# Fourier weight tiles loaded with 128 rows instead of 127, and the two special rows in one load

## The chip, the cores and the metric

The kernel runs on one core of one Trainium2 chip. The metric is the time of one launch in microseconds (us), as the device reports it; of several runs the median counts. Engines are named as the profile names them: PE (matmul; PEld is its weight load), DVE (vector), ACT (scalar), POOL (GpSimd) and SP, whose queue here issues nearly all DMAs.

## The reference, cut to what matters

A trunk of two layers works on 16 meta tokens and 1024 tokens of width 1024, L = 1040 positions in all. Each layer normalises, projects into four groups (pooling, Fourier, state space, attention), mixes each group, gates it, and adds an output projection of all four to the residual. The change touches the Fourier group alone:

```python
def fourier_mix(u, w):
    mixed = jnp.fft.fft2(u.astype(jnp.float32), axes=(1, 2), norm="ortho").real
    return jnp.einsum("blc,cd->bld", mixed.astype(u.dtype), w)
```

## The kernel before, in words

The transform over the 512 channels and the weight `w` (512x512) are both linear, so the kernel first folds them into one: `fft_tables` (L404) multiplies a cosine and sine table with `w`, and what it leaves, the tiles `s.mt` and the row `s.mn`, is the right side of the transform over channels in `fft_inner` (L443). Since the tables have symmetries, `fft_tables` needs only sums and differences of rows of `w`: row m with row 512 - m, and so on. The host lays out `w` for this as `fw`: four tiles of 128 rows per layer, tiles 0 and 2 in rising order, tiles 1 and 3 in the falling order of their partners. The partners of rows 0 and 256 are missing, so row 0 of tile 1 holds the special row 128 and row 0 of tile 3 the special row 384.

In each layer `fft_tables` does this:

- it loads the tables `cc` (L407) and `cn` (L408) into a `big` tile;
- it loads the four weight tiles into the left half of four `big` tiles (L415), all 128 rows of tiles 0 and 2, but only rows 1 to 127 of tiles 1 and 3, whose row 0 DVE sets to zero (L414);
- it loads the special rows, row 0 of tiles 1 and 3, into a tile of two rows, one DMA each (L417, L418);
- DVE forms tile 0 plus and minus tile 1, then tile 2 plus and minus tile 3 (L423), and from these four the next four (L427);
- PE multiplies the tables with these (L432), and the two special rows with their entries of `cn` (L434); ACT and DVE split the product into a high and a low part (L128, L129).

All of a layer is written as generators that yield after each small step; `weave` runs several of them in turn, in fixed proportions, and a scheduler then orders each engine's instructions. Each engine works through its list strictly in order, and waits on semaphores where an instruction needs another engine or a DMA. A `big` tile (30 of them) has to be read for the last time before a load may write it anew, so each L415 waits for a matmul of PE.

`fft_tables` runs while two other generators do. One is the last part of attention, `att_main` (scores at L655 and L656, exponentials on ACT at L658, sums of them on DVE and POOL at L666 and L668, weighted values at L678, the sums' ones-matmul at L687). The other is the output projection of the pooling group, `outproj` (L330): for each of eight weight tiles (loaded at L205, split by ACT at L128 and DVE at L129) and three chunks of positions it loads the residual into an `sms` tile (L338; there are four such tiles), multiplies on PE into a PSUM bank (L132 to L134), adds the bank to the `sms` tile on DVE (L352), which frees the bank, and stores the tile to `hd` in DRAM (L353), which frees the `sms` tile. Ahead of it stands the load of the pooling group's result (L325), split by the same L128 and L129.

Of the kernel before, what the change touches and what calls it, by code (L numbers as in the profile page):

```python
# [52 lines left out]
def hybrid_trunk(ctx: ExitStack, tc: tile.TileContext, io, out, depth=DEPTH):  # L53
    nc = tc.nc
# [10 lines left out]
    vecs = const.tile([128, DEPTH * NV], F32, name="vecs")  # L65
# [31 lines left out]
    def big(dt=F32):  # L97
        return bigp.tile([128, SLOT], dt, name=nm("big"), tag="big", bufs=NBIG)
# [18 lines left out]
    def ps(tag):  # L117

        ring = [tag] * PSB[tag] + [x for x, t in zip(("y0", "y1", "y2"), phase["spare"]) if t == tag]
        turn[tag] = (turn[tag] + 1) % len(ring)  # L120
        x = ring[turn[tag]]
        return psp.tile([128, 512], F32, name=nm("ps" + x), tag=x, bufs=PSB.get(x, 1))
# [4 lines left out]
    def split(hi, lo, src):  # L127
        nc.scalar.copy(hi, src)  # L128
        nc.vector.tensor_tensor(lo, src, f(hi), op=ALU.subtract)  # L129
# [274 lines left out]
    def fft_tables(l, s):  # L404

        cc = big()
        nc.sync.dma_start(cc[:, :513], io["cc"])  # L407
        nc.sync.dma_start(cc[0:2, 513:513 + 257], io["cn"])  # L408
        t = [big() for _ in range(4)]
        a = [x[:, 0:512] for x in t]  # L410

        for i in range(4):
            if i % 2:
                nc.vector.memset(a[i][0:1], 0.0)  # L414
            nc.sync.dma_start(a[i][i % 2:128], io["fw"][l, i, i % 2:128])  # L415
        w2 = big()[0:2, 0:512]
        nc.sync.dma_start(w2[0:1], io["fw"][l, 1, 0:1])  # L417
        nc.sync.dma_start(w2[1:2], io["fw"][l, 3, 0:1])  # L418
        yield
        b = [x[:, 512:1024] for x in t]  # L420
        for i in range(4):
            x = 2 * (i % 2)
            nc.vector.tensor_tensor(b[i], a[x], a[x + 1], op=(ALU.add, ALU.subtract)[i // 2])  # L423

        for i, op in enumerate((ALU.add, ALU.subtract, ALU.subtract, ALU.add)):
            x = 2 * (i // 2)
            nc.vector.tensor_tensor(a[i], b[x], b[x + 1], op=op)  # L427
        s.mt, s.mn = [], big()[0:1, 0:512]
        for i, (m0, m1, x, extra) in enumerate(((0, 128, 0, 0), (129, 257, 1, None), (257, 385, 2, None), (385, 513, 3, 129), (128, 129, 0, 128))):
            n = m1 - m0  # L430
            p = ps("xx")[0:n]
            nc.tensor.matmul(p, cc[:, m0:m1], a[x], start=True, stop=extra is None)  # L432
            if extra is not None:
                nc.tensor.matmul(p, cc[0:2, 513 + extra:513 + extra + n], w2, start=False, stop=True)  # L434
            if n == 128:
                r = big(F32R)
                s.mt.append((r[:, 0:512], r[:, 528:1040]))
                split(*s.mt[-1], p)
            else:
                nc.scalar.copy(s.mn, p)  # L440
            yield
# [581 lines left out]
    for l in range(depth):  # L1023
# [38 lines left out]
        def stage(gen, steps, n):  # L1062
            run(weave((gen, steps), (islice(fill2, n), n)))
        phase["spare"] = SPARE[2]
        tabs = fft_tables(l, s)
        next(tabs)
        run(islice(fill2, 1))
# [90 lines left out]
def _layout(i):  # L1158
    a = {k: np.asarray(v) for k, v in i.items()}
    w_in = a["w_in"]  # L1160
    o_up, o_gp, o_uf, o_gf, o_x, o_z, o_dt, o_q, o_k, o_v, o_ga = 0, 512, 1024, 1536, 2048, 3072, 3584, 3600, 4112, 4240, 4368
    starts = [o_up + 128 * t for t in range(4)] + [o_gp + 128 * t for t in range(4)]
    cols = [np.arange(s0, s0 + 128) for s0 in starts]
    cols += [o_uf + np.arange(0, 256, 2), o_uf + np.arange(1, 256, 2)]
    cols += [o_uf + np.r_[256, np.arange(510, 256, -2)], o_uf + np.arange(511, 256, -2)]
    starts = [o_gf + 128 * t for t in range(4)] + [o_x + 128 * t for t in range(8)] + [o_z + 128 * t for t in range(4)]
    starts += [o_q + 128 * t for t in range(4)] + [o_k, o_v] + [o_ga + 128 * t for t in range(4)]
    cols += [np.arange(s0, s0 + 128) for s0 in starts]
    cols = np.concatenate(cols)
    w1 = w_in[:, :, cols].reshape(DEPTH, 8, 128, NT, 128).transpose(0, 3, 2, 1, 4)  # L1170
    perm = np.array([0, 2, 4, 6, 1, 3, 5, 7])
    r40 = np.concatenate([perm] * 4 + [8 + perm])
    wdt = np.zeros((DEPTH, 1024, 64), np.float32)
    wdt[:, :, :40] = w_in[:, :, o_dt + r40]
    wdt = wdt.reshape(DEPTH, 8, 128, 64).transpose(0, 2, 1, 3)
    w2 = a["w_out"].reshape(DEPTH, 4, 4, 128, 8, 128).transpose(0, 1, 4, 3, 2, 5)
    fw = a["fourier_w"]
    rows = np.concatenate([np.arange(128), [128], np.arange(511, 384, -1), np.arange(256, 128, -1), [384], np.arange(257, 384)])
    fw = fw[:, rows].reshape(DEPTH, 4, 128, 512)
    r128 = np.resize(r40, 128)  # L1180
    v = []
    for l in range(DEPTH):
        col = lambda x: x.reshape(-1, 128).T
        v += [col(a["norm_w"][l]), col(a["pool_scale"][l]), col(a["conv_w"][l].reshape(-1)), col(a["conv_b"][l]),
              col(a["ssd_norm_w"][l]), col(np.repeat(a["d_skip"][l], 64)), col(np.tile(a["q_norm_w"][l], 2)), col(np.tile(a["k_norm_w"][l], 2)),
              a["dt_bias"][l].reshape(-1)[r128][:, None], a["a_log"][l].reshape(-1)[r128][:, None]]
    xT = np.concatenate([a["meta_tokens"], a["x"][0]], 0).T
    r = {"xT": xT, "w1": w1, "wdt": wdt, "w2": w2, "fw": fw, "pool_w": a["pool_w"], "vecs": np.concatenate(v, 1)}
    r.update(_constants())
    return {k: np.ascontiguousarray(x) for k, x in r.items()}  # L1190

# [13 lines left out]
```

## Time and profile before

| what | us |
|---|---|
| median of 3 timed runs | 2136.37 |
| lowest and highest | 2135.49, 2142.13 |
| the profiled execution's own time | 2144.23 |
| its span, first to last instruction | 2142.5 |
| PE busy in it | 2007.5 |
| DVE busy | 1398.6 |
| ACT busy | 1012.6 |

The profile is of one execution, and its stretches are given in us from the start of its span. A busy time is the union of an engine's instructions; an instruction in the list of one engine comes with the idle time before it and what ended that. `fft_tables` starts near 712 us in layer 0 and near 1766 us in layer 1. SP's instructions are issues: a DMA moves its bytes after them.

### The profile page before, as it was taken

To read this page: it belongs to the slowest core of one execution; us is meant where nothing else is said; L and a number is where in the kernel's file an instruction comes from. 1 tells how busy PE (TensorE), PEld (TensorE's weight loads), DVE (VectorE), ACT (ScalarE), POOL (GpSimd) and SP (SyncE) were. 2 spreads that over 40 slices of the span, in tenths; PEclk is the share of its full clock that TensorE was granted. 3 is DMA by queue.
4 is the path that set the end of the run, shared out by engine and by line. 5 is a ranking of instruction groups with operands and counts; after the bars stand their busy time and mean duration, and the time that the engine had idled before them with its cause. 6 is when DMAs were issued, how large, how long until landed. Compare 5 with 4: busy or idle time off the path is not lost.

```text
span 2142.5 us, 33401 instructions
## 1 busy us (share of the span) xinstructions
PE 2007.5 (94%) x11880; PEld 1756.2 (82%) x11880; DVE 1398.6 (65%) x2785; ACT 1012.6 (47%) x2191; POOL 464.2 (22%) x465
## 2 busy tenths in 40 slices
PE   6999999999999898888889999999999998979888
PEld 5898988688899568877779988877888995878878
DVE  5575547767664455689795655476675635476996
ACT  5534344453542546356464344435534433463652
POOL 2012122031110210245230221221311103012550
PEclk9999999999999999999999999998999999988999
DMA  4322222123233477676643221212223344776666
GB/s 138 99 74 62 64 63 57 43 76 97 91 127 104 135 210 246 193 187 191 169 123 116 66 67 54 73 44 72 68 98 102 117 129 127 241 217 180 175 184 195
DMA packets 164605, 261.01 MB, mean 122 GB/s; under 512 B 20878, under 2 KB 113618, under 8 KB 164438
## 3 DMA queue, kind: packets, MB, share of 16 engines
q1 hardware_dynamic: 161782, 249.55, 38.7%
q0 software_dynamic: 2656, 9.33, 1.8%
q8 instruction: 93, 1.52, 0.3%
q14 instruction: 74, 0.61, 0.1%
HBM read 182.91 MB, written 71.67 MB: 119 GB/s over the span
## 4 chain that ended last, share of the span: by engine, by line
PE 68%; DVE 14%; DMA 9%; ACT 4%; issue 3%; POOL 2%; SPq 1%; DVEq 0%; POOLq 0%; ACTq 0%
PE psmm L132 11%; PE psmm L133 10%; PE psmm L134 10%; PE pspv L678 6%; PE psy L132 5%; PE psy L133 5%; PE psy L134 5%; PE psy L655 2%; PE psy L626 2%; PE psy L656 2%; DMA hd<-sms 2%; DVE bb L883 1%; PE pssc L655 1%; DMA big<-ecd 1%; PE pssc L626 1%
## 5 line engine op out<-in xcount | busy, mean ns | idle before, releaser
L132 PE MATMUL psmm<-big,wh 128*128 128x346 f32 (+2 forms) x1920 | 645.5, 337 | 42.0 <-DVE sms L352 19.2
L133 PE MATMUL psmm<-big,wh 128*128 128x346 f32 (+2 forms) x1920 | 633.8, 330 | 7.6 <-DVE big L129 4.7
L134 PE MATMUL psmm<-big,wl 128*128 128x346 f32 (+2 forms) x1920 | 628.2, 327 | 1.3 <-DVE wl L129 1.3
L132 PEld LDWEIGHTS psmm<-big,wh 128*128 128x128 f32 x1920 | 370.8, 193 | 88.0 <-issue 29.3
L133 PEld LDWEIGHTS psmm<-big,wh 128*128 128x128 f32 x1920 | 371.0, 193 | 17.8 <-DVE big L129 7.2
L134 PEld LDWEIGHTS psmm<-big,wl 128*128 128x128 f32 x1920 | 371.3, 193 | 4.5 <-DVE wl L129 2.4
L668 POOL TENSOR_TENSOR acc<-acc,pf 116x346 f32<-116x346 f32 (+5 forms) x216 | 222.9, 1044 | 701.2 <-ACT pf L658 557.4
L128 ACT CAST wh<-wr 128x512 fp32r<-128x512 f32 (+1 forms) x236 | 145.2, 616 | 268.6 <-PE psmm L133 205.8
L129 DVE TENSOR_TENSOR wl<-wr,wh 128x512 fp32r<-128x512 f32 x232 | 168.4, 730 | 126.6 <-ACT wh L128 125.2
L132 PE MATMUL psy<-big,wh 128*128 128x346 f32 (+2 forms) x672 | 221.8, 330 | 1.1 <-ACT big L128 0.6
L133 PE MATMUL psy<-big,wh 128*128 128x346 f32 (+2 forms) x672 | 217.7, 324 | 3.1 <-DVE big L188 2.0
L134 PE MATMUL psy<-big,wl 128*128 128x346 f32 (+2 forms) x672 | 216.8, 323 | 0.0
L678 PE MATMUL pspv<-pf,vt 116*64 116x346 f32 (+5 forms) x864 | 168.8, 469 | 0.0
L658 ACT ACTIVATE pf<-psy 116x346 f32<-116x346 f32 (+4 forms) x288 | 125.3, 457 | 87.0 <-PE psy L656 84.8
L668 DVE TENSOR_TENSOR acc<-acc,pf 116x346 f32<-116x346 f32 (+5 forms) x120 | 106.7, 889 | 71.5 <-ACT pf L658 51.0
L627 DVE TENSOR_REDUCE mx<-psy 116x1 f32<-116x346 f32 (+3 forms) x272 | 132.7, 511 | 18.5 <-PE psy L626 18.0
L132 PEld LDWEIGHTS psy<-big,wh 128*128 128x128 f32 x672 | 127.2, 189 | 13.3 <-issue 7.6
L133 PEld LDWEIGHTS psy<-big,wh 128*128 128x128 f32 x672 | 127.0, 189 | 6.9 <-DVE big L188 3.1
L134 PEld LDWEIGHTS psy<-big,wl 128*128 128x128 f32 x672 | 127.0, 189 | 0.8
L678 PEld LDWEIGHTS pspv<-pf,vt 116*64 116x64 f32 (+1 forms) x864 | 59.4, 137 | 62.5 <-issue 26.7
L655 PE MATMUL psy<-big,big 128*116 128x346 f32 (+4 forms) x288 | 96.2, 336 | 0.9 <-DVE mx L627 0.8
L627 DVE TENSOR_REDUCE mx<-pssc 128x1 f32<-128x346 f32 (+3 forms) x136 | 69.8, 513 | 41.7 <-PE pssc L626 40.0
(293 smaller groups left out, 3326.7 us busy)
## 6 DMA issues: line engine op xcount, KB each, us to landing
wr<-w SPq DMA_DIRECT2D x248, 256.0 KB
sms<-hd SPq DMA_DIRECT2D x112, 173.0 KB
hd<-sms SPq DMA_DIRECT2D x96, 173.0 KB
bb<-csd SPq DMA_DIRECT2D x40, 338.0 KB
md<-big SPq DMA_DIRECT2D x24, 520.0 KB
gd<-sms SPq DMA_DIRECT2D x64, 173.0 KB
big<-gd SPq DMA_DIRECT2D x16, 520.0 KB
big<-md SPq DMA_DIRECT2D x16, 520.0 KB
```

The lines of the kernel that those rows point to most:

```text
L128: nc.scalar.copy(hi, src)
L129: nc.vector.tensor_tensor(lo, src, f(hi), op=ALU.subtract)
L132: nc.tensor.matmul(out_ps, ah, bh, start=start, stop=False)
L133: nc.tensor.matmul(out_ps, ah, bl, start=False, stop=False)
L134: nc.tensor.matmul(out_ps, al, bh, start=False, stop=stop)
L626: nc.tensor.matmul(p[:qn, :cw], s1[e][:, q0:q0 + qn], k1[:, c0:c0 + cw], start=True, stop=True)
L627: nc.vector.tensor_reduce(mx[:qn, q, e, ci:ci + 1], p[:qn, :cw], axis=AX.X, op=ALU.max)
L655: nc.tensor.matmul(p[:n, :cw], k1[:, k0:k0 + n], s1[e][:, cs], start=True, stop=False)
L656: nc.tensor.matmul(p[:n, :cw], k3[0:65, k0:k0 + n], q2[e][0:65, cs], start=False, stop=True)
L658: nc.scalar.activation(pf[:n, :cw], p[:n, :cw], AF.Exp, scale=0.125)
L668: eng.tensor_tensor(accs[c0, e][:n, :cw], accs[c0, e][:n, :cw], pf[:n, :cw], op=ALU.add)
L678: nc.tensor.matmul(hold["pv"][64 * e:64 * e + 64, :cw], s.vt[:n, k, v, :], pfs[e][:n, :cw], start=(k == 0), stop=(k == len(KTS) - 1))
```

## The change

The host now lays out rows 1 to 127 of the odd tiles as before but a row of zeros as their row 0, and puts the two special rows into an array of their own, `fwn`. The kernel loads all four tiles with 128 rows, without the memsets, and the special rows with one DMA of two rows. What is computed stays the same.

```diff
@@ fft_tables
         for i in range(4):
-            if i % 2:
-                nc.vector.memset(a[i][0:1], 0.0)
-            nc.sync.dma_start(a[i][i % 2:128], io["fw"][l, i, i % 2:128])
+            nc.sync.dma_start(a[i], io["fw"][l, i])
         w2 = big()[0:2, 0:512]
-        nc.sync.dma_start(w2[0:1], io["fw"][l, 1, 0:1])
-        nc.sync.dma_start(w2[1:2], io["fw"][l, 3, 0:1])
+        nc.sync.dma_start(w2, io["fwn"][l])
         yield
@@ _layout
     rows = np.concatenate([np.arange(128), [128], np.arange(511, 384, -1), np.arange(256, 128, -1), [384], np.arange(257, 384)])
+    fwn = fw[:, [128, 384]]
     fw = fw[:, rows].reshape(DEPTH, 4, 128, 512)
+
+    fw[:, 1::2, 0] = 0
```

Below L415 the changed kernel's lines have lower numbers: L415 is L413, the special rows' load is L415, L423 is L420, L427 is L424, L666 and L668 are L663 and L665; lines up to L411 keep theirs. PE's, ACT's and POOL's lists hold the same instructions; on PE 24 matmuls of the projection in layer 1 stand behind one L678 that they stood ahead of, and ACT's and POOL's order is the same. DVE's and SP's lists change near these loads.

On SP in layer 0, from the fourth load of L338 on; `big_7533` and `big_7535` are the odd weight tiles, `big_7542` (now `big_7540`) the special rows, and the tiles `sms` and stores `hd` are the projection's. Before:

```order
L338 DMA sms_7332<-xT 128x348
L415 DMA big_7535<-fw 127x512
L417 DMA big_7542<-fw 1x512
L353 DMA hd_5727<-sms_7275 128x348
L353 DMA hd_5728<-sms_7292 128x346
L353 DMA hd_5729<-sms_7309 128x346
L418 DMA big_7542<-fw 1x512
L338 DMA sms_7361<-xT 128x346
```

And now:

```order
L338 DMA sms_7332<-xT 128x348
L413 DMA big_7535<-fw 128x512
L415 DMA big_7540<-fwn 2x512
L353 DMA hd_5727<-sms_7275 128x348
L353 DMA hd_5728<-sms_7292 128x346
L353 DMA hd_5729<-sms_7309 128x346
L205 DMA wr_8427<-w 128x512
L338 DMA sms_7361<-xT 128x346
```

In the place of the second special row's load stands a weight load of L205, which stood five rows further down.

On DVE in the same place, from the second memset's row on; the first pair of L423 works on tiles `big_7532` and `big_7533`, the second on `big_7534` and `big_7535`. Before:

```order
L414 MEMSET big_7535 1x512
L668 TENSOR_TENSOR acc_6451<-acc_6451,pf_7357 112x346
L423 TENSOR_TENSOR big_7532<-big_7532,big_7533 128x512
L423 TENSOR_TENSOR big_7534<-big_7532,big_7533 128x512
L352 TENSOR_TENSOR sms_7275<-sms_7275,psmm_7277 128x348
L352 TENSOR_TENSOR sms_7292<-sms_7292,psy_7294 128x346
L352 TENSOR_TENSOR sms_7309<-sms_7309,psmm_7311 128x346
L666 TENSOR_TENSOR acc_7406<-pf_7392,pf_7402 116x346
L129 TENSOR_TENSOR wl_8034<-wr_8031,wh_8033 128x512
L668 TENSOR_TENSOR acc_7406<-acc_7406,pf_7416 116x346
L352 TENSOR_TENSOR sms_7332<-sms_7332,psmm_7334 128x348
L423 TENSOR_TENSOR big_7533<-big_7534,big_7535 128x512
```

And now:

```order
L665 TENSOR_TENSOR acc_6451<-acc_6451,pf_7357 112x346
L420 TENSOR_TENSOR big_7532<-big_7532,big_7533 128x512
L420 TENSOR_TENSOR big_7534<-big_7532,big_7533 128x512
L129 TENSOR_TENSOR wl_8031<-wr_8028,wh_8030 128x512
L352 TENSOR_TENSOR sms_7275<-sms_7275,psmm_7277 128x348
L352 TENSOR_TENSOR sms_7292<-sms_7292,psy_7294 128x346
L352 TENSOR_TENSOR sms_7309<-sms_7309,psmm_7311 128x346
L663 TENSOR_TENSOR acc_7406<-pf_7392,pf_7402 116x346
L420 TENSOR_TENSOR big_7533<-big_7534,big_7535 128x512
L665 TENSOR_TENSOR acc_7406<-acc_7406,pf_7416 116x346
L352 TENSOR_TENSOR sms_7332<-sms_7332,psmm_7334 128x348
L420 TENSOR_TENSOR big_7535<-big_7534,big_7535 128x512
```

The memsets are gone, the split of the weight tile (L129) stands ahead of the three L352, and the first half of the second pair stands two rows earlier, ahead of one L668 (now L665) and the fourth L352; its own second half keeps its place.

More of the change, by code (lines that the diff above doesn't have):

```diff
@@ L1187, in _layout @@
     xT = np.concatenate([a["meta_tokens"], a["x"][0]], 0).T
-    r = {"xT": xT, "w1": w1, "wdt": wdt, "w2": w2, "fw": fw, "pool_w": a["pool_w"], "vecs": np.concatenate(v, 1)}
+    r = {"xT": xT, "w1": w1, "wdt": wdt, "w2": w2, "fw": fw, "fwn": fwn, "pool_w": a["pool_w"], "vecs": np.concatenate(v, 1)}
     r.update(_constants())
```

## The prediction

> **What bounds the kernel now.** I read the page first, for what sets the end.
>
> ```profile
> span 2142.5 us, 33401 instructions
> PE 2007.5 (94%) x11880; PEld 1756.2 (82%) x11880; DVE 1398.6 (65%) x2785; ACT 1012.6 (47%) x2191; POOL 464.2 (22%) x465
> PE 68%; DVE 14%; DMA 9%; ACT 4%; issue 3%; POOL 2%; SPq 1%; DVEq 0%; POOLq 0%; ACTq 0%
> ```
>
> PE is busy for 94% of the span, so a change counts only where PE stands still, or runs slowly, because of what the change touches. The touched lines run once a layer, near 718 and 1772 us. The view of single lines gives the loads of L415 and who waits for them; the rows under it are the DMA list's, the four loads of 256.0 KB (128 rows) and the four of 254.0 KB (127 rows).
>
> ```profile
> L415 SPq DMA_DIRECT2D big<-fw x8: 279/592/4922, 717.5 to 1780.1; - x8
>   DVE big L423: 22.0, 3
> big<-fw SPq DMA_DIRECT2D x4, 256.0 KB
> big<-fw SPq DMA_DIRECT2D x4, 254.0 KB
> ```
>
> DVE waits 22.0 us in all for these loads. Whether PE waits with it, the timelines of DVE, PE and SP around layer 0's loads tell (start, us, what, and in brackets the idle time before and who ended it).
>
> ```profile
> 720.60 0.48 DVE L414 MEMSET big<- 1x512 f32 x1
> 721.01 2.46 DVE L129 TENSOR_TENSOR big<-sms,big 128x346 fp32r<-128x346 f32 x4
> 723.53 0.48 DVE L414 MEMSET big<- 1x512 f32 x1
> 723.94 0.44 DVE L668 TENSOR_TENSOR acc<-acc,pf 112x346 f32<-112x346 f32 x1
> 732.67 1.29 DVE L423 TENSOR_TENSOR big<-big,big 128x512 f32<-128x512 f32 x2 [8.29 <-DMA big<-fw]
> 733.88 0.51 DVE L352 TENSOR_TENSOR sms<-sms,psmm 128x348 f32<-128x348 f32 x1
> 735.59 0.68 DVE L129 TENSOR_TENSOR wl<-wr,wh 128x512 fp32r<-128x512 f32 x1
> 745.48 1.47 DVE L423 TENSOR_TENSOR big<-big,big 128x512 f32<-128x512 f32 x2 [6.65 <-DMA big<-fw]
> ```
> ```profile
> 721.51 0.43 PE L133 MATMUL psmm<-big,wh 128*128 128x346 f32 x1 [0.77 <-DVE big L129]
> 725.87 0.80 PE L678 MATMUL pspv<-pf,vt 116*64 116x346 f32 x4
> 734.44 0.66 PE L132 MATMUL psmm<-big,wh 128*128 128x348 f32 x1 [7.77 <-DVE sms L352]
> ```
> ```profile
> 717.55 5.77 SPq L415 DMA_DIRECT2D big<-fw  x3
> 723.42 3.28 SPq L338 DMA_DIRECT2D sms<-xT  x4
> 726.75 0.68 SPq L415 DMA_DIRECT2D big<-fw  x1
> 727.48 9.28 SPq L417 DMA_DIRECT2D big<-fw  x1
> 738.22 0.51 SPq L418 DMA_DIRECT2D big<-fw  x1
> ```
>
> The next rows are of SP's view: the last of the three L415 by itself, and who ended SP's longest waits (us in all, times, longest).
>
> ```profile
> 718.40 4.92 SPq L415 DMA_DIRECT2D big<-fw  x1
> SPq L338 <- DMA hd<-sms: 9.5, 2, 7.2
> SPq L415 <- PE psmm L132: 4.9, 1, 4.9
> ```
>
> So: the first pair of L423 stands in DVE's order ahead of L352, the add that empties a PSUM bank of the output projection. The pair waits for the first 127-row load until 732.67; L352 comes after it; PE, which needs that bank, stands still for 7.77 us. The stretches of the next view (length, busy time of each engine, granted clock, DMA share, GB/s) show the same in both layers, what PE does right after, and what the DMA engines do meanwhile.
>
> ```profile
> 726.67:734.44 7.77, 0.00 (x1) 0.00 (x0) 1.77 (x4) 0.00 (x0) 0.64 (x1) 0.58 0.20 66
> 734.44:738.09 3.65, 3.65 (x13) 3.65 (x14) 2.26 (x5) 0.00 (x0) 0.00 (x0) 0.50 0.16 57
> 738.09:752.60 14.51, 14.51 (x80) 8.41 (x79) 7.60 (x12) 5.93 (x15) 6.07 (x7) 1.00 0.42 132
> 1780.74:1788.23 7.49, 0.00 (x2) 0.00 (x1) 1.76 (x4) 0.00 (x0) 0.64 (x1) 0.62 0.20 67
> 1788.23:1792.86 4.63, 4.63 (x16) 4.63 (x17) 2.79 (x6) 0.00 (x0) 0.00 (x0) 0.50 0.28 100
> 729.00:732.50 3.50, 0.00 (x0) 0.00 (x0) 0.00 (x0) 0.00 (x0) 0.00 (x0) 0.50 0.07 25
> 739.90:745.30 5.40, 5.40 (x30) 3.00 (x30) 0.00 (x0) 2.77 (x7) 3.12 (x4) 1.00 0.07 25
> ```
>
> While DVE waits for either 127-row load, the 16 DMA engines are busy to 0.07, which is one in sixteen, and move 25 GB/s. A load of 254 KB at 25 GB/s takes 10.4 us, and the second follows the first: the 127-row loads each run on one DMA engine. The Trainium skill says so too (DMA: Bandwidth & Descriptors, "Why a DMA increments its semaphore by 16 and not by 1"): a DMA is spread over the largest number of engines up to 16 that divides its row count, 16 for 128 rows and one for 127; the trace agrees.
>
> **The change part by part.**
>
> *The two odd loads get 128 rows.* Nothing in the trace shows a 128-row `fw` load landing by itself; the nearest are the 256 KB weight loads and 173 KB loads on the chain of waits:
>
> ```profile
> 17.30 3.19 DMA wr<-w
> 2102.23 4.01 DMA wr<-w
> 708.07 2.31 DMA sms<-md
> 1761.01 3.27 DMA sms<-md
> ```
>
> The first odd load is issued before 718.40, where the third L415 starts, so it lands by 722.4 at 4.01 us. DVE reaches the pair at 724.38 (723.94 + 0.44). The wait of 8.29 us goes whole. Next late is the first L352's own input, an `sms` load of L338 issued at 723.42: at 2.31 to 3.27 us it lands at 725.7 to 726.7. DVE is by then through with the pair and with the L129 that now stands behind it (724.38, less 0.82 for the two memsets, + 1.29 + 0.68 = 725.5). L352 takes 0.51 and PE follows 0.05 later (734.44 behind 733.88 + 0.51), so PE starts at 726.3 to 727.3; its work before the stall ended at 726.67 (725.87 + 0.80). What stays of the stall is 0 to 0.6 us by these rows, and 1.3 if the load takes 4.01. I take 0.6 in each layer: 7.2 of 7.77 and 6.9 of 7.49, together **14.1 us**; bounds 12.7 and 15.3.
>
> The Trainium skill (the same page, "Anatomy of one DMA — SWDGE (gpsimd) path") fits 2.0 us plus bytes at 436 GB/s to loads that GpSimd issues; an estimate from it for 173 KB is 2.4 us, by which the stall would be gone whole and the sum 1.2 us larger. No row here has that path with this size.
>
> *The slow clock behind the stall.* PE restarts at a granted clock of 0.50 and does 3.65 us of work at it in layer 0, 4.63 us in layer 1; at 1.00 they take half, so **1.8 and 2.3 us, 4.1 in all**, go with the stall. Bounds: 0 (if what stays of the stall still pulls the clock down) and 4.1.
>
> The Trainium skill (TensorE: Matmul & The Clock Gate, "Part 1: The HAM clock gate") has the half clock set by a free-running window of about 3.4 us of idleness, and warns against fitting a fixed cold count; by it the cold stretch may fall elsewhere, and this term would be anything from 0 to its full size.
>
> *The four memsets (L414) go.* Each holds DVE 0.41 us (720.60 to 721.01, 723.53 to 723.94). The first delays the L129 for which PE waits 0.77: it counts, 0.4 a layer, **0.8 us**. The second lies between L129 and the pair, where DVE now has to wait for L338 anyway: nothing. Bounds 0 and 1.6.
>
> *The second odd load (the third `fw` pair's wait, 6.65 us on DVE).* Booked at nothing: PE is busy for 14.51 of 14.51 us from 738.09 on, across this wait. In the new order that wait stands two rows earlier, ahead of L668's add and the fourth L352. The load is issued after the four L338, at about 726.4, and lands by 730.4 at 4.01 us, some 2 us after DVE is there; behind it stand one L668 and the fourth L352, and PE waited for neither before 752.60. Cover: those 14.5 us of PE work.
>
> *SP.* One special-row load replaces two. The first of them held SP for 9.28 us, against 0.51 for its twin; it stood behind both one-engine loads. Then SP waited 7.2 us more before an L338, for an `hd` store that shares the busy engine. That frees SP by up to 16 us a layer, but PE was not waiting for what SP issued next (14.51 of 14.51), so nothing is booked. The weight load of L205 now goes out five rows earlier, ahead of two L338; it waits for a cast of ACT that was long done:
>
> ```profile
> 723.99 0.62 ACT L128 CAST wh<-wr 128x512 fp32r<-128x512 f32 x1 [1.89 <-PE psmm L133]
> ```
> Bounds for SP and order together: a gain or a loss of 1 us a layer.
>
> **Sum.** 14.1 + 4.1 + 0.8 = 19.0 us. The profiled execution took 2144.23 us (span 2142.5, 1.7 around it); it becomes 2125.2. The median of the three timed runs, 2136.37, is 7.9 below the profiled one; I take the same 19.0 from it: **2117.4 us**. Everything after each stall is released by PE's own progress, so I let the gain pass to the end undiminished. With all bounds at their worst (12.7 + 0 + 0 - 2) it is 10.7 us, 2125.7; at their best (15.3 + 4.1 + 1.6 + 2) 23.0 us, 2113.4.
>
> **The rivals.**
>
> *The loads come late on SP.* The third `fw` load keeps SP for 4.92 us waiting for a PE read, with all four L338 behind it; that stays. If full-width loads in flight push the first L338 to land 2.3 us later than I take, 2.9 us of each stall remain, and with them the half clock, which was down by 729.00, 2.3 us into the stall. For it: 256 KB more on all 16 engines just ahead. Against: a 256 KB load lands whole within 3.19 us, fixed part and all, and the four rows of landings above differ by only 1.7 us. Gain then 19.0 - 4.6 - 4.1 = 10.3 us: 2126.
>
> *The change does not widen the transfer.* If the slow rate came from the source or the row size and not from the count of rows, the loads still take 10.4 us. For it: DVE's wait does not tell the 128-row load from the 127-row one. Against: a share of 0.07 with 128-row loads of the same 2 KB rows landing in 3.19. Then only the memsets go, and the moved third pair blocks L668 until 746: 2136, give or take 3.
>
> *Slower: PE gets long half-clock stretches.* The clock is not always lost to idleness: in layer 1's attention PE is busy 52.59 of 53.60 us at a mean clock of 0.85, while the same stage of layer 0 has 0.97.
>
> ```profile
> 374.90:428.50 53.60, 50.26 (x250) 36.49 (x250) 40.21 (x111) 26.57 (x58) 4.76 (x5) 0.97 0.15 43
> 1446.20:1499.80 53.60, 52.59 (x265) 42.28 (x265) 36.53 (x82) 31.36 (x66) 8.14 (x8) 0.85 0.23 72
> ```
>
> A stage at 0.85 instead of 0.97 costs 0.12 x 53.6 = 6.4 us. Shifted by 9 us and with its rest gone, layer 0's side and what follows could fall into such stretches. It needs three to eat the gain, and from four on it is slower by over 0.3%: 19.0 - 4 x 6.4 = -6.6, 2143. Against: the 14.51 us of unbroken PE work above hold 1.00, and no such run of stretches has a cause in this change.
>
> **How the numbers follow.** A measurement of this kernel tells about 0.3% (6.4 us; the three runs span 2135.49 to 2142.13) from no change. Chances: forecast 0.84 (2113 to 2123), loads late 0.09 (2123 to 2130), no widening 0.04, slower 0.03. Predicted 2117.4. The range reaches from 2112, a little past the best bounds for the spread of the runs, to 2127, which takes in the late loads at their price. Faster by over 0.3% is below 2130: 0.92; within 0.3%: 0.05; slower: 0.03.
>
> **What would show it.** Right: no idle time above 1.3 us on PE before the first L132 of the projection near 726 and 1779; DVE's first pair (then L420) with no idle time from `fw`; the granted clock at 1.00 through both places; no stretch at 0.07 DMA share and 25 GB/s; the one special-row load on SP under 1 us. Wrong in the first rival's way: PE idle before that L132, ended by L352, and L352 by `sms`. Wrong in the second's: the rows of 25 GB/s are still there. Wrong in the third's: both stalls gone, and slices of lower PEclk elsewhere. If all the signs hold and the span falls by much less than 17 us, then the gain was given back later and my step from the stall to the end is the false one.

## The result, and the profile after

Six timed runs of each on one chip gave 2121.75 us (2117.97 to 2127.52) against 2137.61 for the kernel before: a ratio of 0.9925, 95% interval 0.9904 to 0.9946, which is 16.0 us less (11.5 to 20.5). A second comparison, among the experiments below, gave 0.9898 (0.9881 to 0.9915), 21.8 us less (18.2 to 25.5). The 19.0 us of the prediction lie in both intervals, near the upper end of the first and the lower end of the second. The us less are worked out from the ratio, which is not the quotient of the two medians, so they differ from the difference of the medians (15.9 and 20.2 us here). The profiled execution took 2122.54 us (before: 2144.23).

The page of the changed kernel, first lines:

```profile
span 2120.8 us, 33393 instructions
...
PE 1995.3 (94%) x11880; PEld 1747.7 (82%) x11880; DVE 1396.7 (66%) x2781; ACT 1012.3 (48%) x2191; POOL 461.1 (22%) x465
```

The span is 21.7 us shorter and PE is busy for 12.2 us less with the same 11880 matmuls: part of the gain is idle time, part is a faster clock. Around layer 0's loads, DVE's timeline (lines behind the change are three lower than before, so L423 is now L420, L668 is L665):

```profile
724.11 0.51 DVE L665 TENSOR_TENSOR acc<-acc,pf 112x346 f32<-112x346 f32 x1
724.54 1.28 DVE L420 TENSOR_TENSOR big<-big,big 128x512 f32<-128x512 f32 x2
725.74 0.68 DVE L129 TENSOR_TENSOR wl<-wr,wh 128x512 fp32r<-128x512 f32 x1
726.34 0.51 DVE L352 TENSOR_TENSOR sms<-sms,psmm 128x348 f32<-128x348 f32 x1
...
728.74 0.69 DVE L420 TENSOR_TENSOR big<-big,big 128x512 f32<-128x512 f32 x1
```

No row has a bracket: DVE waits neither for the first pair's loads (8.29 us before) nor for the second odd load (6.65 before). PE's timeline in the same place:

```profile
722.21 0.43 PE L133 MATMUL psmm<-big,wh 128*128 128x346 f32 x1 [0.29 <-DVE big L129]
...
726.59 0.80 PE L675 MATMUL pspv<-pf,vt 116*64 116x346 f32 x4
727.32 0.42 PE L132 MATMUL psmm<-big,wh 128*128 128x348 f32 x1
```

The first L132 of the projection, which stood 7.77 us for L352, follows the matmul ahead of it with no idle time at all. The L133 that waits for L129 now waits 0.29 us instead of 0.77, since no memset stands ahead of that L129. SP's timeline, layer 0:

```profile
718.72 1.37 SPq L413 DMA_DIRECT2D big<-fw  x3
722.19 2.35 SPq L338 DMA_DIRECT2D sms<-xT  x4
724.59 0.42 SPq L413 DMA_DIRECT2D big<-fw  x1
725.07 0.28 SPq L415 DMA_DIRECT2D big<-fwn  x1
```

Two holds of SP are gone, not one. The special-row load takes 0.28 us where the first of its forerunners took 9.28. And the three `fw` loads take 1.37 us where they took 5.77: the third of them no longer takes 4.92. The stretches around both places (length, busy time of PE, PEld, DVE, ACT, POOL, then granted clock, DMA share and GB/s):

```profile
726.59:734.36 7.77, 7.77 (x43) 5.94 (x42) 7.02 (x13) 2.68 (x8) 2.57 (x3) 1.00 0.74 211
1764.00:1787.00 23.00, 22.39 (x121) 14.54 (x120) 18.71 (x29) 10.88 (x28) 11.80 (x13) 1.00 0.55 163
```

Where PE stood still for 7.77 us with the DMA engines at 0.20, it now does 43 matmuls at full clock with the DMA engines at 0.74. In layer 1 PE is busy 22.39 of 23.00 us, also at 1.00.

Where the difference of the two profiled executions arose shows when rows that stand at the same point of the program are set side by side: layer 0's first `fw` load, the L463 (now L460) behind the Fourier tables, an L757 (now L754) in layer 1's attention, then the first two again in layer 1. Before (L415's first row is 717.55, quoted in the prediction):

```profile
781.10 0.69 DVE L463 TENSOR_TENSOR big<-big,big 1x521 fp32r<-1x521 f32 x1 [0.41 <-ACT big L461]
1437.16 0.37 DVE L757 TENSOR_TENSOR big<-ce,big 40x208 f32<-40x208 f32 x1
1771.65 5.63 SPq L415 DMA_DIRECT2D big<-fw  x3
1834.85 0.69 DVE L463 TENSOR_TENSOR big<-big,big 1x521 fp32r<-1x521 f32 x1 [0.42 <-ACT big L461]
```

After:

```profile
771.92 0.69 DVE L460 TENSOR_TENSOR big<-big,big 1x521 fp32r<-1x521 f32 x1 [0.41 <-ACT big L458]
1432.17 0.37 DVE L754 TENSOR_TENSOR big<-ce,big 40x208 f32<-40x208 f32 x1
1761.89 1.48 SPq L413 DMA_DIRECT2D big<-fw  x3
1813.45 0.69 DVE L460 TENSOR_TENSOR big<-big,big 1x521 fp32r<-1x521 f32 x1 [0.44 <-ACT big L458]
```

The changed kernel stands 1.2 us later at 717.55 and then 9.2, 5.0, 9.8 and 21.4 us earlier; at the end it is 21.7. So layer 0's place gave 10.4 us and layer 1's 11.6. Between them 4.2 us were given back by 1437, and 4.8 came again between 1437 and 1771. The second of these shows in the stretches around that attention stage; before:

```profile
1437.90:1441.30 3.40, 2.87 (x13) 1.64 (x13) 2.96 (x9) 0.80 (x4) 0.21 (x1) 1.00 0.00 0
1441.30:1461.80 20.50, 20.11 (x50) 10.92 (x49) 15.47 (x46) 7.88 (x23) 4.80 (x5) 0.50 0.05 12
```

After, at the same point of the program:

```profile
1432.90:1436.30 3.40, 2.87 (x13) 1.65 (x13) 2.97 (x9) 0.81 (x4) 0.21 (x1) 1.00 0.02 2
1436.30:1456.80 20.50, 18.54 (x91) 12.85 (x90) 18.43 (x57) 9.91 (x30) 4.53 (x5) 1.00 0.08 19
```

The profiled execution of before ran PE at half clock for 20.5 us there, 50 matmuls where the other did 91. That is some 5 us of the 21.7. No line of the change runs there, and of the experiments below the kernel with 122 rows has the same stretch in its profile (busy for 20.11 of 20.50 us, 50 matmuls, at 0.52); the other profiles do not.

### The profile page after: what moved, and what is told of

Same layout as the page of the kernel before. It is cut to its first block, busy times and chain, and to the rows that moved or that the text cites. A ratio compares the mean times of both kernels' runs of the same rounds, so it can differ in the third digit from the quotient of the medians.

```text
span 2120.8 us, 33393 instructions
## 1 busy us (share of the span) xinstructions
PE 1995.3 (94%) x11880; PEld 1747.7 (82%) x11880; DVE 1396.7 (66%) x2781; ACT 1012.3 (48%) x2191; POOL 461.1 (22%) x465
## 4 chain that ended last, share of the span: by engine, by line
PE 66%; DVE 12%; DMA 10%; ACT 5%; issue 4%; POOL 3%; SPq 1%; DVEq 0%; POOLq 0%; ACTq 0%
PE psmm L132 10%; PE psmm L133 10%; PE psmm L134 10%; PE pspv L675 6%; PE psy L132 5%; PE psy L133 5%; PE psy L134 5%; PE psy L652 2%; PE psy L623 2%; DMA hd<-sms 2%; PE psy L653 2%; DMA big<-md 2%; DMA sms<-hd 2%; DMA sms<-md 1%; PE pssc L652 1%
## 5 line engine op out<-in xcount | busy, mean ns | idle before, releaser
L132 PE MATMUL psmm<-big,wh 128*128 128x346 f32 (+2 forms) x1920 | 643.5, 336 | 29.3 <-ACT sms L349 10.3
L133 PE MATMUL psmm<-big,wh 128*128 128x346 f32 (+2 forms) x1920 | 632.3, 329 | 6.0 <-DVE big L129 3.2
L132 PEld LDWEIGHTS psmm<-big,wh 128*128 128x128 f32 x1920 | 369.6, 193 | 74.7 <-issue 29.2
L133 PEld LDWEIGHTS psmm<-big,wh 128*128 128x128 f32 x1920 | 369.3, 192 | 15.6 <-DVE big L129 5.4
L665 POOL TENSOR_TENSOR acc<-acc,pf 116x346 f32<-116x346 f32 (+5 forms) x216 | 220.8, 1035 | 673.4 <-ACT pf L655 534.0
L129 DVE TENSOR_TENSOR wl<-wr,wh 128x512 fp32r<-128x512 f32 x232 | 170.1, 737 | 126.6 <-ACT wh L128 125.3
L132 PE MATMUL psy<-big,wh 128*128 128x346 f32 (+2 forms) x672 | 221.6, 330 | 1.0 <-ACT big L128 0.4
L133 PE MATMUL psy<-big,wh 128*128 128x346 f32 (+2 forms) x672 | 217.5, 324 | 2.6 <-DVE big L188 1.5
L665 DVE TENSOR_TENSOR acc<-acc,pf 116x346 f32<-116x346 f32 (+5 forms) x120 | 108.8, 907 | 77.1 <-ACT pf L655 50.8
L132 PEld LDWEIGHTS psy<-big,wh 128*128 128x128 f32 x672 | 126.9, 189 | 12.9 <-issue 7.4
L133 PEld LDWEIGHTS psy<-big,wh 128*128 128x128 f32 x672 | 126.8, 189 | 6.0 <-DVE big L188 2.3
```

The lines of the kernel that those rows point to most:

```text
L132: nc.tensor.matmul(out_ps, ah, bh, start=start, stop=False)
L133: nc.tensor.matmul(out_ps, ah, bl, start=False, stop=False)
L665: eng.tensor_tensor(accs[c0, e][:n, :cw], accs[c0, e][:n, :cw], pf[:n, :cw], op=ALU.add)
```

## The experiments

The theory under test: a load runs on as many DMA engines as share its rows evenly, so 127 rows run on one; DVE's first pair waits for the first such load, and PE with it. The rivals: it is not the count of rows but where the load starts; it is the second odd load, or what SP is held from, that costs; it is the two small loads.

**The odd tiles in two pieces, 112 and 15 rows.**

```diff
             if i % 2:
                 nc.vector.memset(a[i][0:1], 0.0)
-            nc.sync.dma_start(a[i][i % 2:128], io["fw"][l, i, i % 2:128])
+                nc.sync.dma_start(a[i][1:113], io["fw"][l, i, 1:113])
+                nc.sync.dma_start(a[i][113:128], io["fw"][l, i, 113:128])
+            else:
+                nc.sync.dma_start(a[i], io["fw"][l, i])
```

> The kernel before, with its memsets and both special-row loads, but each odd tile loaded in two pieces: rows 1 to 112 (112 = 16 x 7 rows) and rows 113 to 127 (15 rows). Theory (a load runs on as many DMA engines as share its rows evenly, so 127 rows run on one): both pieces spread, the stalls of 7.77 and 7.49 us go as in the changed kernel and only the memsets' 0.8 us stay: 15 to 19 us below the kernel before, no stretch at 0.07 DMA share, and SP no longer held for 9.28 us at the first special row. Rival (the slow rate comes from the source's offset of one row or from the tile's start at partition 1, not from the count): the first piece still starts there and is still slow, 224 KB at 25 GB/s take 9.2 us, so the stalls shrink by about 1 us each: 0 to 3 us below the kernel before. Rival (what helps is the missing memsets and the moved order, not the transfer): 0 us.

Measured: 2121.83 us against 2139.96, ratio 0.9902 (0.9876 to 0.9928), 21.0 us less; by the medians 18.1, in the expected range, which the ratio passes. The first half of DVE's first pair (L426 in this kernel), the second memset, and the stretches over both places:

```profile
719.59 0.67 DVE L426 TENSOR_TENSOR big<-big,big 128x512 f32<-128x512 f32 x1
723.84 0.48 DVE L414 MEMSET big<- 1x512 f32 x1
```
```profile
717.90:740.00 22.10, 21.99 (x121) 14.83 (x122) 18.91 (x28) 9.73 (x25) 15.17 (x12) 1.00 0.51 150
1758.00:1782.00 24.00, 23.97 (x129) 15.70 (x128) 20.47 (x29) 9.56 (x23) 13.70 (x12) 1.00 0.46 136
```

This half of the pair does not wait, PE is busy for 21.99 of 22.10 us, and the whole gain is there with the host's layout, the memsets and the two small loads untouched. The first piece starts at the same row and the same partition as the 127-row load did. So it is the count of rows, and not the place or the zero row. (The place is not the changed kernel's to the row: the residual loads L338 stand ahead of the third `fw` load, and one half of the first pair, not both, ahead of L352. Nor is it the order that took the wait away: the 112 rows were issued at 714.52, 5.1 us ahead of the pair at 719.59, and at 25 GB/s their 224 KB would have taken 9.2 us.) In layer 1 DVE waits 0.96 us for a piece of the second odd load, across which PE is busy.

**Only tile 1 whole; only tile 3 whole.** The first, with `r = int(i == 3)`; the second has 1 and 3 exchanged. Both are shown against the kernel before; in both `fwn` is laid out as in the change, and the special rows are two loads.

```diff
-            if i % 2:
+            if i == 3:
                 nc.vector.memset(a[i][0:1], 0.0)
-            nc.sync.dma_start(a[i][i % 2:128], io["fw"][l, i, i % 2:128])
+            r = int(i == 3)
+            nc.sync.dma_start(a[i][r:128], io["fw"][l, i, r:128])
...
-        nc.sync.dma_start(w2[0:1], io["fw"][l, 1, 0:1])
-        nc.sync.dma_start(w2[1:2], io["fw"][l, 3, 0:1])
+        nc.sync.dma_start(w2[0:1], io["fwn"][l, 0:1])
+        nc.sync.dma_start(w2[1:2], io["fwn"][l, 1:2])
...
+    fw[:, 1, 0] = 0
```

> Only tile 1 whole with its zero row; tile 3 still 127 rows behind a memset; the two special rows by two loads from the small array. Theory (the first pair's wait is all that PE feels; the second odd load is hidden behind PE's own work): 15 to 19 us below the kernel before, with a wait of some 5 to 10 us left on DVE at the third pair, ended by fw, and PE idle under 1 us there; SP still held some us at a special row behind the one 127-row load. Rival (the cover goes with the stall: the third pair now stands ahead of the fourth L352, and everything comes 8 us earlier, so PE meets this wait): PE idle 3 to 7 us a layer before an L132 near 730 to 740 and again at half clock behind it, so only 4 to 10 us below the kernel before.

Measured: 2123.38 us, ratio 0.9903 (0.9876 to 0.9931), 20.8 us less (16.6 by the medians). DVE's third pair, SP, and the stretches behind each place:

```profile
737.19 1.29 DVE L424 TENSOR_TENSOR big<-big,big 128x512 f32<-128x512 f32 x2 [7.14 <-DMA big<-fw]
```
```profile
718.56 1.37 SPq L416 DMA_DIRECT2D big<-fw  x3
...
724.77 3.76 SPq L418 DMA_DIRECT2D big<-fwn  x1
```
```profile
727.50:752.00 24.50, 24.50 (x127) 15.42 (x125) 14.97 (x23) 8.84 (x21) 10.63 (x10) 1.00 0.40 124
732.00:737.00 5.00, 5.00 (x29) 2.93 (x30) 0.00 (x0) 2.86 (x8) 3.61 (x4) 1.00 0.07 25
1768.00:1800.00 32.00, 32.00 (x160) 20.29 (x160) 20.00 (x33) 11.22 (x26) 13.03 (x13) 1.00 0.45 126
```

DVE waits 7.14 us for the load that is still narrow (again 0.07 and 25 GB/s), and PE is busy for 24.50 of 24.50 us across it. The cover that the prediction named for the second odd load holds even with the stall gone. (Later in layer 1, at 1809.28, PE waits 3.33 us for a load of `md` that lands 29 us after the narrow one. The changed kernel waits 0.79 us there, and the kernel with two special loads, which has no narrow load, 2.05. I do not put this wait down to the narrow load, but no run settles it.)

> Only tile 3 whole; tile 1 still 127 rows behind a memset; the two special rows by two loads from the small array. Theory: the first pair still waits for its 127-row load, PE still stands 7 to 8 us in each layer and restarts at half clock: 0 to 3 us below the kernel before, though DVE's 6.65 us wait at the third pair is gone and SP is held less at the special row. Rival (SP's hold and the second load carry a share of the gain, since SP's later loads go out up to 16 us earlier): 4 to 10 us below. In sum the gains of this kernel and of the one with tile 1 alone should make the whole change's gain if neither hides the other.

Measured: 2139.12 us, ratio 0.9995 (0.9976 to 1.0014). PE and SP in layer 0:

```profile
734.17 0.66 PE L132 MATMUL psmm<-big,wh 128*128 128x348 f32 x1 [7.99 <-DVE sms L352]
```
```profile
717.64 4.93 SPq L416 DMA_DIRECT2D big<-fw  x3
...
726.53 0.70 SPq L418 DMA_DIRECT2D big<-fwn  x1
```

The stall is there whole (8.01 us in layer 1), and so is the time. SP's hold of 9.28 us at the special row is down to 0.70, and that is worth nothing. So the first odd load carries the gain; the second odd load and the freed SP add nothing that these runs can tell.

**The odd tiles in two pieces, 122 and 5 rows.** As the first experiment, with 123 in place of 113.

```diff
+                nc.sync.dma_start(a[i][1:123], io["fw"][l, i, 1:123])
+                nc.sync.dma_start(a[i][123:128], io["fw"][l, i, 123:128])
```

> As the kernel before, but each odd tile loaded as rows 1 to 122 (122 = 2 x 61 rows) and rows 123 to 127 (5 rows). Theory (engines share the rows evenly, the largest count up to 16 that divides them): two engines, about 50 GB/s, 244 KB in 4.9 us instead of 10.4; the first piece lands 5 to 6 us earlier than the 127-row load, DVE waits 1 to 3 us at the first pair, and PE's stall falls from 7.77 to 0.5 to 2.5 us a layer with most of the clock kept: 10 to 17 us below the kernel before; while it runs alone the DMA share is about 0.13. Rival (a load either spreads over all 16 engines or falls to one): 244 KB on one engine take 9.8 us, the stalls stay within 1 us of what they were: 0 to 3 us below. Rival (any load without the first row spreads once it is not 127 rows, as with 112): no wait at all and the full 15 to 19 us. The Trainium skill (DMA: Bandwidth & Descriptors, "Why a DMA increments its semaphore by 16 and not by 1") has the rule of the largest divisor, by which this load gets two engines.

Measured: 2128.79 us, ratio 0.9936 (0.9915 to 0.9958), 13.7 us less (11.2 by the medians; the profiled execution took 2135.55). DVE, PE, and stretches:

```profile
729.55 0.69 DVE L426 TENSOR_TENSOR big<-big,big 128x512 f32<-128x512 f32 x1 [3.95 <-DMA big<-fw]
```
```profile
730.73 0.66 PE L132 MATMUL psmm<-big,wh 128*128 128x348 f32 x1 [2.93 <-DVE sms L352]
...
1778.46 0.65 PE L132 MATMUL psmm<-big,wh 128*128 128x332 f32 x1 [1.96 <-DVE sms L352]
```
```profile
730.73:734.20 3.47, 3.47 (x13) 3.47 (x14) 2.68 (x6) 0.00 (x0) 0.00 (x0) 0.54 0.55 162
738.00:740.00 2.00, 2.00 (x13) 1.24 (x14) 0.00 (x0) 1.91 (x6) 1.82 (x3) 1.00 0.13 51
1778.46:1782.00 3.54, 3.54 (x13) 3.54 (x14) 2.69 (x6) 0.00 (x0) 0.00 (x0) 0.53 0.51 177
```

Between one engine and sixteen lie two: where the second odd piece runs alone the share is 0.13 and the rate 51 GB/s, twice the 0.07 and 25. The Trainium skill's rule (DMA: Bandwidth & Descriptors, "Why a DMA increments its semaphore by 16 and not by 1") gives 122 rows two engines; this trace agrees. The wait falls from 8.29 to 3.95 us and the stalls to 2.93 and 1.96; the wait and layer 0's stall are longer than I had expected (1 to 3 and 0.5 to 2.5). That most of the clock would be kept was wrong: PE restarts at 0.54 and 0.53 for some 3.5 us, so 3.3 of the 4.1 us of the clock term stay (3.47 x 0.46 + 3.54 x 0.47). The stalls alone shrank by 4.8 and 5.5 us. The time lies between the two kernels, as the theory has it and neither rival.

**The special rows in two loads, the rest as changed.**

```diff
-        nc.sync.dma_start(w2, io["fwn"][l])
+        nc.sync.dma_start(w2[0:1], io["fwn"][l, 0:1])
+        nc.sync.dma_start(w2[1:2], io["fwn"][l, 1:2])
```

> The changed kernel, but with the special rows as two loads of one row each from the small array. Theory (SP's 9.28 us at the first special row came from the two 127-row loads ahead of it, not from the one-row load itself): each special-row load holds SP under 1 us, and the time is that of the changed kernel within 3 us, about 16 us below the kernel before. Rival (the one small load of two rows is itself part of the gain): SP is held again for some us at the first special row and the time is 2 to 6 us above the changed kernel's.

Measured: 2119.59 us against 2139.25, ratio 0.9903 (0.9886 to 0.9920). SP:

```profile
724.74 0.28 SPq L415 DMA_DIRECT2D big<-fwn  x1
...
728.47 0.30 SPq L416 DMA_DIRECT2D big<-fwn  x1
```

Neither load holds SP, and the time is the changed kernel's. The merging of the two rows into one load is worth nothing that these runs can tell.

**The changed kernel again.**

> The changed kernel once more, for a second profile and a narrower ratio. Theory (the two places gave about 20 us, and the 3 to 4 us that the span fell short of it are half-clock stretches that lie elsewhere in another execution, not a new wait): again no PE idle time before the first L132 at the two places, the time 15 to 19 us below the kernel before, and the total of half-clock time in the profile different from the first one's by some us with the span following it. Rival (part of the gain is given back at a fixed later wait): the same 3 to 4 us are lost at the same place behind layer 0's stall, about 2119 to 2122 us in both profiles, and the ratio stays near 0.9925 within 0.001.

Measured: 2119.04 us against 2139.25, ratio 0.9898 (0.9881 to 0.9915). Its DVE and PE at layer 0's place:

```profile
726.21 1.41 DVE L129 TENSOR_TENSOR wl<-wr,wh 128x512 fp32r<-128x512 f32 x1
```
```profile
728.10 0.43 PE L132 MATMUL psmm<-big,wh 128*128 128x348 f32 x1 [0.82 <-DVE sms L352]
```

Here 0.82 us of the stall stay, where the first profile had none, so the expectation of no idle time was missed by this much. It is not a load that comes late: DVE has no idle time ahead of this L352, but the L129 before it takes 1.41 us where it took 0.68 in the first profile. The other question was whether the 4.2 us that were given back between the two places are a fixed wait. The rows of the two points, in this profile and then in that of the kernel with two special loads, which differs by one small DMA:

```profile
772.28 0.69 DVE L460 TENSOR_TENSOR big<-big,big 1x521 fp32r<-1x521 f32 x1 [0.41 <-ACT big L458]
...
1432.73 0.37 DVE L754 TENSOR_TENSOR big<-ce,big 40x208 f32<-40x208 f32 x1
```
```profile
770.35 0.69 DVE L461 TENSOR_TENSOR big<-big,big 1x521 fp32r<-1x521 f32 x1 [0.41 <-ACT big L459]
...
1427.43 0.37 DVE L755 TENSOR_TENSOR big<-ce,big 40x208 f32<-40x208 f32 x1
```

The repeat is 8.8 us ahead of the kernel before at the first point and 4.4 at the second: it gave back 4.4 us again, as the rival had it and not the theory. The kernel with two special loads is 10.8 ahead and then 9.7: it gave back 1.0. But the kernel with tile 3 alone whole, which keeps both stalls, loses as much between these points:

```profile
779.53 0.69 DVE L464 TENSOR_TENSOR big<-big,big 1x521 fp32r<-1x521 f32 x1 [0.41 <-ACT big L462]
...
1438.93 0.37 DVE L758 TENSOR_TENSOR big<-ce,big 40x208 f32<-40x208 f32 x1
```

It is 1.6 us ahead of the kernel before and then 1.8 behind, a loss of 3.3 us with next to nothing to give back; the kernels with 112 rows and with tile 1 whole, which both gained, lost 1.4 and 3.9. So the loss does not follow the gain. One part of the difference is in the clock; the changed kernel first, then the one with two special loads, in the last stage of layer 0:

```profile
1084.00:1094.00 10.00, 8.27 (x38) 7.16 (x38) 7.61 (x13) 3.78 (x7) 2.58 (x3) 0.83 0.65 179
```
```profile
1084.00:1094.00 10.00, 9.48 (x56) 8.68 (x55) 8.94 (x17) 5.99 (x12) 2.07 (x2) 1.00 0.53 154
```

The changed kernel has a half-clock stretch there, worth some 1.7 us (0.17 of 10 us), the other none. In both it stands behind the same idle time of PE, 1.74 us before 1086.77 and 1083.51: equal idle times cost the clock in one execution and not in the other. So some two fifths of what was given back is such a stretch, which a kernel with the same work need not have; the rest I could not assign, and whether the changed kernel always loses it these profiles leave open. The time was 20.2 us less in the medians, a little more than the 15 to 19 that I expected.

## Why the prediction was right, step by step

- **The stall.** Right in place, cause and size. Booked 14.1 us with 0.6 left per layer; the first profile has nothing left in either layer (15.26 us gone), the second 0.82 in layer 0. The first experiment shows the cause (112 rows from the same start: no wait), and the pair of single tiles shows that it is the first odd load alone.
- **The residue, and one false step behind it.** I wrote that the third `fw` load keeps SP for 4.92 us for a PE read and that this stays. It did not stay. The row that named PE as the one that ended the wait does not hold: with tile 1 whole the three loads take 1.37 us whatever tile 3 is; with tile 1 narrow they take 4.93 with tile 3 whole and 5.77 with it narrow. SP was held because the load issued just before was a one-engine load. With the hold gone the four L338 start 2.4 us earlier against the program (722.19 instead of 723.42, in an execution that stood 1.2 us later there), which fits that L352 found its input in place. Nor did any load of L413 then wait long for a matmul of PE to free its tile: all three were out in 1.37 us. The error was on the safe side, and it also takes away the ground of the first rival, the loads that come late.
- **The half clock.** Right: 4.1 us booked, and both places run at 1.00. The middle case of 122 rows shows that shorter stalls can cost it too: 2.93 and 1.96 us were each followed by 3.4 us at half clock. They need not: with tile 1 whole, PE stood for 1.98 us before 766.30 and went on at 1.00.
- **The memsets.** Booked 0.4 a layer on PE's wait before an L133. That wait fell from 0.77 to 0.29, 0.5 us. The timed runs cannot tell it: the kernel that keeps all four memsets has the changed kernel's ratio (0.9902 against 0.9898).
- **The second odd load, SP and the order.** Booked at nothing; shown by the two single-tile kernels, 0.9903 and 0.9995.
- **The gain passes to the end.** As an account of the 19.0 us it held, but not because nothing happened in between. The two places gave 10.4 and 11.6 us in the pair of profiles, of which 9.4 and 9.6 were booked; the terms as measured (15.3 + 4.1 + 1.0) make 20.4, and 1.6 us of the 22.0 stay without a name. Between the places some 4 us went, over half of them open, and a kernel that kept its stalls lost 3.3 there as well; some 5 came with a half-clock stretch in which no line of the change runs. That the profiles' 21.7 us and the forecast lie so close is in part luck, since these two nearly cancel.
- **The slower rival.** The mean clock of 0.85 in layer 1's attention, on which I built it, came from the one stretch of 20.5 us shown above, which the changed kernel's profile lacks. A price per stage had been read from a single occurrence. Its direction, that such stretches move the time by several us either way, is borne out.

## What to carry to other kernels

Look at the row count of every DMA on which something waits: a load of 127 rows ran on one engine at 25 GB/s, 122 rows on two at 51, and with 112 or 128 rows PE met no such stall (at most 0.82 us before that L132, and not from these loads), so a zero row from the host, or a load cut into 112 and 15, takes away the same stall. A DMA share of 1/16 or 2/16 with an engine waiting is the sign of it. Whether it is worth anything is read at the bound engine: of two equally slow loads here one cost about the whole 20 us and the other, 7 us of waiting on DVE, nothing that the runs can tell, because PE had 24.5 us of work across it.

## What the runs showed of the hardware

- The issue of a DMA right behind a one-engine load holds the issuing queue: 4.92 us for the `fw` load behind the first 127-row load; for the special row behind the second, 9.28 us with the first narrow too and 3.76 with it whole (9.49 and 2.04 in layer 1); 0.28 to 0.70 where no such load stood right ahead. A trace's releaser (here PE) can be wrong for such a wait.
- A half-clock stretch lasted 3.4 us or a multiple of it: 3.4 at both places of the 122-row kernel, 10.2 in layer 0 of the kernel before (727.88 to 738.12), 20.5 in its layer 1 (1441.27 to 1461.75). The Trainium skill (TensorE: Matmul & The Clock Gate, "Part 1: The HAM clock gate") ties the half clock to a free-running window of about 3.4 us; these lengths agree with it, but 3.4 us of idle time was not needed, as the stall of 1.96 us shows.
- The same idle time does not always cost the clock. Near 1090 us PE stands for 1.73 to 1.75 us in each of the eight profiles; the mean clock of the 3 us behind it is 0.54 to 0.58 in three of them (the changed kernel twice, and tile 1 whole) and 1.00 in five. So the half-clock stretches of a single profile do not price a kernel.
- Half the clock came also with PE busy: 20.11 of 20.50 us at 0.50 in the kernel before, behind 3.40 us with PE busy for 2.87 at full clock and the DMA engines at rest. The changed kernel ran the same 3.40 us (2.87 busy) and stayed at 1.00. What decides between these two executions no run here shows.
